# A norm's gain folded into the weights it feeds, on Pool, and Pool's additions and products handed to VectorE

## The chip, the cores and the metric

The kernel runs on one core of a Trainium2 chip. Its time is device microseconds from the first to the last instruction of one execution. The profile names the engines: PE is TensorE's matrix multiply, PEld its weight loads, DVE is VectorE, ACT is ScalarE, POOL is GpSimd ("Pool" below), SP is SyncE, which issues most of the DMAs.

## The reference: what is computed

A bidirectional encoder with two layers; S = 1024 tokens, D = 1024, a hidden width of 2816, all in fp32. Each layer mixes tokens (a Fourier group, windowed attention, attention on a memory), adds the normed result to x, and then runs a gated feed-forward block:

```python
y = jnp.concatenate([...], axis=-1) @ w_out[l]
x = x + _rmsnorm(y, g_post_mix[l])

h = _rmsnorm(x, g_pre_ffn[l])                   # x * rsqrt(mean(x*x) + eps) * g
gate, up = jnp.split(h @ w_ffn_in[l], 2, axis=-1)
f = (jax.nn.silu(gate) * up) @ w_ffn_out[l]
x = x + _rmsnorm(f, g_post_ffn[l])
```

## The kernel before

Every operand of a matmul is split into a high and a low part in a reduced fp32 format (`split`, L151 a cast on ACT for the high part, L152 a subtraction on DVE for the low one), and a product is formed from three matmuls. The two large products of the feed-forward block, "ffn_in" (h @ w_ffn_in) and "ffn_out", are done by a scheme with seven block products in place of eight: rows of x and columns of weights are cut in two, sums and differences of the blocks are multiplied, and results are added up.

**From the mixer to ffn_in (the transition).** The last stage of the mixer goes over eight token tiles of 128 rows, t = 0 to 7. `out` multiplies by w_out ("mo"), adds the parts (L1041 on DVE, with a factor `grs` from Pool), forms the residual (L337 and L338 on DVE, L337 multiplying by the row g_post_mix) and norms the row: L289 squares and sums it on ACT, L291 stores x to DRAM, two small Pool operations (L210 `nrsv`, L212 `nrs`) make the factor r, and L294 on DVE computes x * r * g_pre_ffn. Both gains are rows of 1024 values that a DMA spreads over all partitions, 512 KB each, at slots 48 and 52 of the arena. `Blocks.tile` then transposes the row on PE ("hTp", L1066), ACT copies the result (L1067), and `Blocks.sum` and `Blocks.last` build the block sums on DVE (L1084, L1096, L1097) and their splits. Blocks 2 and 4 need only token tiles 0 to 3, the others need tiles 4 to 7 too.

**ffn_in.** For each of 11 pairs p of hidden blocks there are two "quads", the gate's and the up's, each of seven products (names qy, qz, qx, qw; L1137, 12 matmuls of 512 columns each) in the order 2, 4, 5, 1, 6, 7, 3. `Quad.load` brings two raw tiles (512 KB each) of w_ffn_in; `weights` forms a sum of two parts of them on DVE (L1127) and splits it. The ring of split weight tiles holds eight. The raw tiles of pair 0 lie at slots 32, 0, 16 and 20, those of the later pairs at 44, 48, 52 and 56, and so a load waits for what lay there. `step` collects the products: ACT copies one out of PSUM (L1142), Pool adds to it (L1157) or subtracts from it (L1163), DVE does the sums with an operand in PSUM (L1158, L1169, L1172, L1173). `up_out` multiplies the up quad by silu of the gate quad (four L1189) and forms sums for ffn_out (L1199, L1201, L1203), which go to DRAM ("actd"). In all pairs but the last, Pool does two of the L1189, two of the L1199 and the L1203. `scaled` (L342), which multiplies a weight tile by one column of factors on Pool, is there already for the weights of other stages.

Every engine has one queue of instructions. Their order is set by a scheduler when the kernel is built, from its own estimates of times, so it shifts around an edit.

Of the kernel before, what the change touches and what calls it, by code (L numbers as in the profile page):

```python
# [11 lines left out]
F32 = mybir.dt.float32  # L12
# [3 lines left out]
AF = mybir.ActivationFunctionType  # L16
ALU = mybir.AluOpType
AX = mybir.AxisListType

P = 128  # L20
D = 1024
S = 1024
NT = S // P
NK = D // P
# [44 lines left out]
def tile_encoder(ctx: ExitStack, tc: tile.TileContext, T, C, out):  # L69
# [51 lines left out]
    def run(k, n, step):  # L121
        return Ring(*[k + i * step for i in range(n)])
# [40 lines left out]
                self.i += 1  # L163


    const = cp.tile([P, 1376], F32, name="const")
    used = [0]

    def cst(*shape):
# [28 lines left out]

    ggT = cst(DEPTH * NK)
    gpT = cst(DEPTH * NK)  # L200
    rx = cst(NT)
    nsink = cst(DEPTH, 8)
    psink = cst(DEPTH, 8)
# [11 lines left out]
    def gain(row, g):  # L215
        nc.sync.dma_start(g, row.partition_broadcast(P))
        return g
# [6 lines left out]
        nc.scalar.copy(dst, pt)  # L224

    def prep():
        tmp = run(6, 10, 1)
        gains_T(ggT, T["g_grp"], tmp(P))
        nc.sync.dma_start(psink, T["sink"].rearrange("l h -> (l h)").partition_broadcast(P).rearrange("p (l h) -> p l h", l=DEPTH))
        nc.vector.tensor_scalar_mul(nsink, psink, -1.0)  # L230

        pi = tmp(P, dt=I32)[:NT]
        nc.sync.dma_start(pi, T["positions"].rearrange("o (t p) -> (o t) p", p=P))
        pf = tmp(P)[:NT]
        nc.vector.tensor_copy(pf, pi)
        pp_ = ps([NT], "posT")
        nc.tensor.transpose(pp_, pf, ident[:NT, :NT])
        pos = sm(NT, "pos")
        nc.vector.tensor_copy(pos, pp_)
        invf = tmp(HD // 2)  # L240
        nc.sync.dma_start(invf, C["invf"].partition_broadcast(P))
        H = HD // 2
        shp = [NT, H]
        ang = tmp(*shp)
        nc.vector.tensor_tensor(
            out=ang, in0=pos[:, :, None].to_broadcast([P, NT, H]),
            in1=invf[:, None, :].to_broadcast([P, NT, H]), op=ALU.mult,
        )


        BIG = 1.5 * 2.0 ** 23
        two_pi = 2 * math.pi
        p_parts, p_rest = _bits_split(two_pi * 4096, [7] * 6)
        q_parts, q_rest = _bits_split(two_pi, [12] * 3)

        def count(src, unit):
            n = tmp(*shp)
            nc.vector.tensor_scalar(out=n, in0=src, scalar1=1.0 / unit, scalar2=BIG, op0=ALU.mult, op1=ALU.add)
            nc.vector.tensor_scalar_sub(n, n, BIG)
            return n  # L260

        def less(dst, n, part, src):
            nc.vector.scalar_tensor_tensor(out=dst, in0=n, scalar=-part, in1=src, op0=ALU.mult, op1=ALU.add)

        n1 = count(ang, two_pi * 4096)
        for part in p_parts[:3]:
            less(ang, n1, part, ang)
        est = tmp(*shp)
        less(est, n1, sum(p_parts[3:]), ang)
        n2 = count(est, two_pi)  # L270
        less(ang, n2, q_parts[0], ang)
        less(ang, n1, p_parts[3], ang)
        less(ang, n2, q_parts[1], ang)
        less(ang, n1, p_parts[4], ang)
        less(ang, n1, p_parts[5], ang)
        less(ang, n2, q_parts[2], ang)
        lim = float(np.nextafter(np.float32(math.pi), np.float32(0)))
        nc.vector.tensor_scalar(out=ang, in0=ang, scalar1=lim, scalar2=-lim, op0=ALU.min, op1=ALU.max)
        nc.scalar.activation(SS[:, :, H:HD], ang, AF.Sin)
        mag = tmp(*shp)  # L280
        nc.vector.scalar_tensor_tensor(out=mag, in0=ang, scalar=-1.0, in1=ang, op0=ALU.mult, op1=ALU.max)
        nc.scalar.activation(CC, mag, AF.Sin, bias=halfpi[:, 0:1], scale=-1.0)
        nc.vector.tensor_scalar_mul(SS[:, :, 0:H], SS[:, :, H:HD], -1.0)


    def norm_x(x, g, h=None, keep=None):

        ss = sm(1, "nss")
        nc.scalar.activation(junks(D // 2).bitcast(BF16) if h is None else h, x, AF.Square, accum_out=ss)  # L289
        if keep is not None:  # L290
            nc.scalar.dma_start(keep, x)  # L291
        h = x if h is None else h
        r = rsqrt_mean(ss, D, 1, "nrs")
        nc.vector.scalar_tensor_tensor(out=h, in0=x, scalar=r[:, 0:1], in1=g, op0=ALU.mult, op1=ALU.mult)  # L294
        return h

    def token_scale(x, t):
# [188 lines left out]
    class Mix:  # L486
# [525 lines left out]

        def out_gains(self):
            self.gpost = gain(T["g_post_mix"][self.l], at(48, D))
            self.gffn = gain(T["g_pre_ffn"][self.l], at(52, D))
            junks.ks, sqs.ks, es_ring.ks = (58,), (56, 56), (36, 39, 42, 45)
            self.prepped, self.xf = {}, {}

# [11 lines left out]
        def out(self, t, x1):  # L1030

            x, f = self.xf.pop(t)
            (hi, lo), rs = self.prepped.pop(t)
            for n in range(2):
                ns = slice(n * 512, n * 512 + 512)
                pt = ps([512], "mo")
                acc = Acc(pt, 4)
                for i in range(4):
                    w = self.woa[2 + i]
                    acc.add(hi[:, i], lo[:, i], w[0][:, ns], w[1][:, ns])  # L1040
                nc.vector.scalar_tensor_tensor(  # L1041
                    out=f[:, ns], in0=pt, scalar=rs[:, 0:1], in1=f[:, ns], op0=ALU.mult, op1=ALU.add
                )
            residual(x, f, self.gpost)
            return norm_x(x, self.gffn, f, x1)

# [52 lines left out]
    class Quad:  # L1101


        def __init__(self, l, c0, hb):
            self.hb, self.c0 = hb, c0
            self.w = T["w_ffn_in"][l]

        def load(self):
            self.raw = []
            for kg in range(2):  # L1110
                r = qws(4, 2, P)
                nc.sync.dma_start(
                    r, self.w[kg * 512 : kg * 512 + 512, self.c0 : self.c0 + 256].rearrange("(k p) (j c) -> p k j c", p=P, c=P)
                )
                self.raw.append(r)

        def weights(self, i):
# [27 lines left out]
        def step(self, i):  # L1145

            if i == 2:
                self.y = ps([512], "qy", "pT")
                self.product(self.y, 2, True)
                self.s2 = self.snap(self.y)  # L1150
            if i == 4:
                self.product(self.y, 4, False)
            if i == 5:
                self.z = ps([512], "qz", "av")
                self.product(self.z, 5, True)
                self.v = self.snap(self.z)
                nc.gpsimd.tensor_tensor(out=self.v, in0=self.v, in1=self.s2, op=ALU.add)  # L1157
                nc.vector.tensor_tensor(out=self.s2, in0=self.y, in1=self.v, op=ALU.subtract)  # L1158
            if i == 1:
                self.x = ps([512], "qx", "sc")  # L1160
                self.product(self.x, 1, True)
                self.s1 = self.snap(self.x)
                nc.gpsimd.tensor_tensor(out=self.s1, in0=self.v, in1=self.s1, op=ALU.subtract)  # L1163
            if i == 6:
                self.w6 = ps([512], "qw", "pd")
                self.product(self.w6, 6, True)
            if i == 7:
                self.product(self.x, 7, False)
                nc.vector.tensor_tensor(out=self.s2, in0=self.x, in1=self.s2, op=ALU.add)  # L1169
            if i == 3:  # L1170
                self.product(self.z, 3, False)
                nc.vector.tensor_tensor(out=self.s1, in0=self.z, in1=self.s1, op=ALU.subtract)  # L1172
                nc.vector.tensor_tensor(out=self.s1, in0=self.w6, in1=self.s1, op=ALU.add)  # L1173
                self.out = (self.s2, self.z, self.y, self.s1)
# [8 lines left out]

    def up_out(q, g, actd, p):

        V, G = nc.vector, nc.vector if p == NFF // 2 - 1 else nc.gpsimd
        a = [acts(512) for _ in range(4)]
        for i, c in enumerate(q.out):
            (G if i in (0, 3) else V).tensor_tensor(out=a[i], in0=c, in1=g[i], op=ALU.mult)  # L1189
        a11, a21, a12, a22 = a  # L1190

        def put(i, s):
            nc.sync.dma_start(actd[i - 1, p], s)

        put(3, a11)
        put(4, a22)
        for i, x, y, eng in ((1, a11, a22, G), (2, a21, a22, V), (5, a11, a12, G)):
            s = acts(512)
            eng.tensor_tensor(out=s, in0=x, in1=y, op=ALU.add)  # L1199
            put(i, s)  # L1200
        V.tensor_tensor(out=a21, in0=a21, in1=a11, op=ALU.subtract)  # L1201
        put(6, a21)
        G.tensor_tensor(out=a12, in0=a12, in1=a22, op=ALU.subtract)  # L1203
        put(7, a12)

    def quads(l, p, hb):
# [297 lines left out]
```

## Time and profile before

| | before |
|---|---|
| runs, us | 2087.84, 2090.29, 2091.57 (median 2090.29) |
| span of the profiled execution, us | 2089.2 |
| mean granted TensorE clock | 0.981 |
| busy: PE, DVE, ACT, POOL, us | 1994.7, 1578.8, 1069.9, 713.1 |
| ffn_in, layer 0 and layer 1, us from the start | 424 to about 843, 1454 to about 1868 |
| transition, layer 0 and layer 1 | about 394 to 424, 1421 to 1454 |

The profiled execution has no other time than its span, which lies within the runs. Times below are microseconds from the span's start. A line number such as L294 is the line of the kernel before; "x44" counts instructions, and in rows of a timeline "[0.44 <-POOL grs L962]" is the idle time of the engine just before, with what ended it.

### The profile page before, as it was taken

The page shows a single profiled execution, that of the slowest core. Times are in us where ns is not written, and L with a number is a line of the kernel's source. Part 1 is how long each engine was busy: PE and PEld are TensorE (multiplying, and loading weights), DVE is VectorE, ACT ScalarE, POOL GpSimd, SP SyncE. Part 2 cuts the span into 40 slices and gives each one's busy share as a digit, 9 for nine tenths or more (in the row PEclk, how much of TensorE's full clock was granted, in tenths as well). Part 3 has the DMA queues.
Part 4 walks back from the last instruction along what each step waited for, and adds up shares of the span by engine and source line. Part 5 has one row for each costly group of instructions (what it writes and reads, how often), then busy time and mean ns, then how long its engine had stood idle before and what let it go on. Part 6 is the DMA issues. An engine that isn't in the chain of part 4 may idle for free.

```text
span 2089.2 us, 28535 instructions
## 1 busy us (share of the span) xinstructions
PE 1994.7 (95%) x9587; PEld 1646.5 (79%) x9587; DVE 1578.8 (76%) x2540; ACT 1069.9 (51%) x2270; POOL 713.1 (34%) x819
## 2 busy tenths in 40 slices
PE   7998999799999999999999979997999999989998
PEld 6876787578888888887788768775788888878886
DVE  5558767898787877778867686579878787778767
ACT  6467777654333333544555677675433333345441
POOL 4344435433333423002523544453343342320002
PEclk9999999999999999999999999998999999999999
DMA  6111132423232333879831122233233232269874
GB/s 211 51 51 61 56 112 91 162 71 101 97 120 87 126 96 116 312 271 328 279 133 45 48 66 86 77 134 118 86 104 114 86 131 96 92 210 343 303 261 151
DMA packets 173347, 286.48 MB, mean 137 GB/s; under 512 B 15464, under 2 KB 73360, under 8 KB 173200
## 3 DMA queue, kind: packets, MB, share of 16 engines
q1 hardware_dynamic: 165136, 265.78, 37.9%
q10 hardware_dynamic: 8064, 18.88, 2.3%
q8 instruction: 75, 1.23, 0.2%
q14 instruction: 72, 0.59, 0.1%
HBM read 218.02 MB, written 66.58 MB: 136 GB/s over the span
## 4 chain that ended last, share of the span: by engine, by line
PE 74%; DVE 9%; DMA 7%; ACT 5%; issue 3%; POOL 2%; SPq 0%; DVEq 0%; ACTq 0%; POOLq 0%
PE fo L1270 13%; PE qx L1137 11%; PE qy L1137 10%; PE qz L1137 10%; PE mo L162 7%; PE qw L1137 5%; PE kvp L162 4%; DVE arena_r L152 3%; PE qp L162 3%; DMA arena_f<-actd 3%; PE zT L162 2%; PE pT L798 1%; ACT arena_r L151 1%; DMA arena_f<-in_w_ffn_out 1%; PE sc L761 1%
## 5 line engine op out<-in xcount | busy, mean ns | idle before, releaser
L151 ACT CAST arena_r<-arena_f 128x512 fp32r<-128x512 f32 (+1 forms) x780 | 443.7, 591 | 632.6 <-PE qz L1137 119.9
L152 DVE TENSOR_TENSOR arena_r<-arena_f,arena_r 128x512 fp32r<-128x512 f32 (+1 forms) x676 | 509.4, 774 | 148.1 <-ACT arena_r L151 136.8
L1270 PE MATMUL fo<-arena_r 128*128 128x512 f32 x1848 | 425.1, 391 | 8.7 <-ACT arena_r L151 7.3
L1270 PEld LDWEIGHTS fo<-arena_r 128*128 128x128 f32 x1848 | 346.6, 188 | 82.4 <-ACT arena_r L151 8.1
L1137 PE MATMUL qy<-arena_r 128*128 128x512 f32 x1056 | 261.9, 397 | 22.3 <-ACT arena_r L151 12.5
L1137 PEld LDWEIGHTS qy<-arena_r 128*128 128x128 f32 x1056 | 201.7, 192 | 66.6 <-ACT arena_r L151 13.3
L1127 DVE TENSOR_TENSOR arena_f<-arena_f 128x512 f32<-128x512 f32 x220 | 205.9, 939 | 8.9 <-issue 2.4
L1137 PE MATMUL qz<-arena_r 128*128 128x512 f32 x704 | 196.6, 389 | 1.1 <-DVE arena_r L152 1.1
L1157 POOL TENSOR_TENSOR arena_f<-arena_f 128x512 f32<-128x512 f32 x44 | 73.9, 1679 | 310.2 <-ACT arena_f L1142 310.2
L1137 PEld LDWEIGHTS qz<-arena_r 128*128 128x128 f32 x704 | 132.1, 188 | 28.9 <-DVE arena_r L152 1.5
L152 POOL TENSOR_TENSOR arena_r<-arena_f,arena_r 128x256 fp32r<-128x256 f32 (+2 forms) x104 | 87.0, 842 | 129.5 <-ACT arena_r L151 84.4
L1137 PE MATMUL qx<-big,arena_r 128*128 128x512 f32 x528 | 127.1, 389 | 1.7 <-ACT arena_f L1142 1.7
L1137 PE MATMUL qx<-arena_r 128*128 128x512 f32 x528 | 127.9, 389 | 0.5 <-ACT arena_r L151 0.5
L1137 PE MATMUL qw<-arena_r 128*128 128x512 f32 x528 | 128.3, 389 | 0.0
L1189 POOL TENSOR_TENSOR arena_f<-arena_f 128x512 f32<-128x512 f32 x40 | 66.7, 1667 | 159.7 <-DVE arena_f L1169 122.4
L1137 PEld LDWEIGHTS qx<-big,arena_r 128*128 128x128 f32 x528 | 99.0, 188 | 22.6 <-ACT arena_f L1142 2.1
L1137 PEld LDWEIGHTS qx<-arena_r 128*128 128x128 f32 x528 | 99.1, 188 | 21.4 <-ACT arena_r L151 0.9
L1137 PE MATMUL qz<-big,arena_r 128*128 128x512 f32 x352 | 115.7, 389 | 0.0
L1137 PEld LDWEIGHTS qw<-arena_r 128*128 128x128 f32 x528 | 99.1, 188 | 20.6
L210 POOL TENSOR_SCALAR rrsv<-rss 128x1 f32<-128x1 f32 x32 | 13.6, 424 | 267.6 <-ACT arena_f L323 210.0
L162 PE MATMUL mo<-big,arena_r 128*128 128x512 f32 x384 | 102.2, 406 | 0.8 <-ACT arena_f L1001 0.8
L162 PE MATMUL mo<-arena_r 128*128 128x512 f32 x384 | 100.7, 403 | 0.9 <-POOL arena_r L152 0.6
(228 smaller groups left out, 3518.3 us busy)
## 6 DMA issues: line engine op xcount, KB each, us to landing
arena_f<-in_w_ffn_out SPq DMA_DIRECT2D x264, 256.0 KB, 4.6
arena_f<-in_w_ffn_in SPq DMA_DIRECT2D x88, 512.0 KB, 3.7
actd<-arena_f SPq DMA_DIRECT2D x154, 256.0 KB, 3.7
arena_f<-actd SPq DMA_DIRECT2D x154, 256.0 KB, 4.5
arena_f<-in_w_in SPq DMA_DIRECT2D x40, 256.0 KB, 3.0
arena_f<-in_x SPq DMA_DIRECT2D x16, 512.0 KB, 5.3
arena_f<-in_w_out SPq DMA_DIRECT2D x32, 256.0 KB, 2.7
pmd<-arena_f ACTq DMA_DIRECT2D x32, 256.0 KB, 2.0
```

Of the source, the lines that this page charges most:

```text
L151: nc.scalar.copy(hi, src)
L152: return (lo_eng or nc.vector).tensor_tensor(out=lo, in0=src, in1=f32(hi), op=ALU.subtract)
L162: mm(self.dst, a, b, start=self.i == 0, stop=self.i == self.n - 1)
L210: nc.gpsimd.tensor_scalar(out=v, in0=ss, scalar1=1.0 / n, scalar2=EPS, op0=ALU.mult, op1=ALU.add)
L761: mm(pt, lhs, self.kst[g][i][:, k0 * P : k1 * P], start=i == 0, stop=i == 1)
L798: nc.tensor.transpose(pT[:, h, :], es_[h // 2][:, h % 2, j * P : j * P + P], ident)
L1127: nc.vector.tensor_tensor(out=s, in0=a, in1=b, op=op)
L1137: mm(pt, a, b, start=start and n == 0, stop=n == 11, skip_group_check=not start)
L1157: nc.gpsimd.tensor_tensor(out=self.v, in0=self.v, in1=self.s2, op=ALU.add)
L1189: (G if i in (0, 3) else V).tensor_tensor(out=a[i], in0=c, in1=g[i], op=ALU.mult)
L1270: mm(pt, ab[:, 0, x, sl], ab[:, 1, y], start=new and first and j == 0, stop=last and j == 2, skip_group_check=not new)
```

## The change

The gain g_pre_ffn no longer multiplies the normed rows. It is brought once, transposed to columns (`gfT`), and Pool multiplies each raw tile of w_ffn_in with it, in four operations of 128x256 a tile (88 tiles, 352 operations). The norm's row is multiplied by r alone, on Pool (`norm_rows`). The g_pre_ffn row at slot 52 is no longer loaded. All tensor-tensors of ffn_in that Pool did are on DVE: 44 of L1157, 44 of L1163, 40 of L1189, 40 of L1199 and 20 of L1203. In the changed kernel lines after 296 have moved by 10 to 12 (L1127 is L1139 there, L1157 is L1169, and `scaled` is L353).

```diff
+    gfT = cst(DEPTH * NK)
...
+        gains_T(gfT, T["g_pre_ffn"], tmp(P))
...
+    def norm_rows(x, h, keep):
+
+        ss = sm(1, "nss")
+        nc.scalar.activation(h, x, AF.Square, accum_out=ss)
+        nc.scalar.dma_start(keep, x)
+        r = rsqrt_mean(ss, D, 1, "nrs")
+        nc.gpsimd.tensor_scalar(out=h, in0=x, scalar1=r[:, 0:1], scalar2=1.0, op0=ALU.mult, op1=ALU.mult)
+        return h
...
-            self.gffn = gain(T["g_pre_ffn"][self.l], at(52, D))
...
-            return norm_x(x, self.gffn, f, x1)
+            return norm_rows(x, f, x1)
...
+                for k in range(4):
+                    scaled(r[:, k], gfT, self.l * NK + 4 * kg + k)
...
-                nc.gpsimd.tensor_tensor(out=self.v, in0=self.v, in1=self.s2, op=ALU.add)
+                nc.vector.tensor_tensor(out=self.v, in0=self.v, in1=self.s2, op=ALU.add)
...
-                nc.gpsimd.tensor_tensor(out=self.s1, in0=self.v, in1=self.s1, op=ALU.subtract)
+                nc.vector.tensor_tensor(out=self.s1, in0=self.v, in1=self.s1, op=ALU.subtract)
...
-        V, G = nc.vector, nc.vector if p == NFF // 2 - 1 else nc.gpsimd
+        V = nc.vector
         a = [acts(512) for _ in range(4)]
         for i, c in enumerate(q.out):
-            (G if i in (0, 3) else V).tensor_tensor(out=a[i], in0=c, in1=g[i], op=ALU.mult)
+            V.tensor_tensor(out=a[i], in0=c, in1=g[i], op=ALU.mult)
...
-        for i, x, y, eng in ((1, a11, a22, G), (2, a21, a22, V), (5, a11, a12, G)):
+        for i, x, y in ((1, a11, a22), (2, a21, a22), (5, a11, a12)):
...
-        G.tensor_tensor(out=a12, in0=a12, in1=a22, op=ALU.subtract)
+        V.tensor_tensor(out=a12, in0=a12, in1=a22, op=ALU.subtract)
```

How the edit changes the order of instructions is shown at layer 0's transition. Pool's queue before, from token tile 7's factor `grs` to the first operations of ffn_in (`nrsv` and `nrs` belong to a norm, `rrsv` and `rrs` to a residual):

```order
L962 TENSOR_TENSOR grs_585_3991<-ms_584_3989,const_77 128x1
L210 TENSOR_SCALAR nrsv_592_4032<-nss_591_4029 128x1
L212 TENSOR_TENSOR nrs_593_4034<-nrsv_592_4032,const_77 128x1
L210 TENSOR_SCALAR rrsv_601_4096<-rss_600_4094 128x1
L212 TENSOR_TENSOR rrs_602_4098<-rrsv_601_4096,const_77 128x1
L210 TENSOR_SCALAR nrsv_604_4105<-nss_603_4102 128x1
L212 TENSOR_TENSOR nrs_605_4107<-nrsv_604_4105,const_77 128x1
L1157 TENSOR_TENSOR arena_f_73<-arena_f_73 128x512 x2
L1163 TENSOR_TENSOR arena_f_73<-arena_f_73 128x512 x2
```

And after the change (L353 is a scaling of a raw tile's quarter, L305 the norm's row of a token tile):

```order
L353 TENSOR_SCALAR arena_f_73<-arena_f_73,const_77 128x256 x4
L211 TENSOR_SCALAR nrsv_593_4035<-nss_592_4032 128x1
L213 TENSOR_TENSOR nrs_594_4037<-nrsv_593_4035,const_77 128x1
L305 TENSOR_SCALAR arena_f_73<-arena_f_73,nrs_594_4037 128x1024
L353 TENSOR_SCALAR arena_f_73<-arena_f_73,const_77 128x256 x4
L211 TENSOR_SCALAR rrsv_602_4099<-rss_601_4097 128x1
L213 TENSOR_TENSOR rrs_603_4101<-rrsv_602_4099,const_77 128x1
L353 TENSOR_SCALAR arena_f_73<-arena_f_73,const_77 128x256 x12
L211 TENSOR_SCALAR nrsv_605_4108<-nss_604_4105 128x1
L353 TENSOR_SCALAR arena_f_73<-arena_f_73,const_77 128x256 x4
L213 TENSOR_TENSOR nrs_606_4110<-nrsv_605_4108,const_77 128x1
L305 TENSOR_SCALAR arena_f_73<-arena_f_73,nrs_606_4110 128x1024
```

Between token tile 6's norm and token tile 7's there now stand 20 scalings; the last four of the twelve wait for a load into the slot that held the g_post_mix row, and the four behind `nrsv` for one into slot 20.

PE's queue before, from token tile 7's transposes to the first products that need them (hTp_612 and hTp_613 are token tile 7's two halves, qy_608 and qy_611 the first products of the two quads):

```order
L1137 MATMUL qy_608_4136<-arena_r_72 128x512 x22
L1137 MATMUL qy_611_4191<-arena_r_72 128x512 x2
L1066 MATMUL hTp_612_4232<-const_77,arena_f_73 128x128 x4
L1066 MATMUL hTp_613_4238<-const_77,arena_f_73 128x128 x4
L1137 MATMUL qy_611_4191<-arena_r_72 128x512 x10
L1137 MATMUL qz_617_4278<-arena_r_72 128x512
L1137 MATMUL qw_619_4315<-arena_r_72 128x512
L1137 MATMUL qz_617_4278<-arena_r_72 128x512 x11
L1137 MATMUL qx_618_4297<-arena_r_72 128x512
L1137 MATMUL qy_611_4191<-arena_r_72 128x512 x12
```

And after:

```order
L1149 MATMUL qy_609_4147<-arena_r_72 128x512 x22
L1149 MATMUL qy_612_4210<-arena_r_72 128x512 x2
L1076 MATMUL hTp_613_4251<-const_77,arena_f_73 128x128 x4
L1149 MATMUL qy_612_4210<-arena_r_72 128x512 x10
L1076 MATMUL hTp_614_4257<-const_77,arena_f_73 128x128 x4
L1149 MATMUL qw_620_4334<-arena_r_72 128x512
L1149 MATMUL qy_612_4210<-arena_r_72 128x512 x12
L1149 MATMUL qw_620_4334<-arena_r_72 128x512 x2
L1149 MATMUL qz_618_4297<-arena_r_72 128x512
L1149 MATMUL qw_620_4334<-arena_r_72 128x512 x9
```

The second qy product of the second quad, 12 matmuls, now stands right behind the first matmul that needs token tile 7, ahead of the bulk of qz and qw.

More of the change, by code (lines that the diff above doesn't have):

```diff
@@ L163, in add @@
                 self.i += 1
-    const = cp.tile([P, 1376], F32, name="const")
+    const = cp.tile([P, 1392], F32, name="const")
     used = [0]
@@ L226, in prep @@
     def prep():
-        tmp = run(6, 10, 1)
+        tmp = run(6, 11, 1)
         gains_T(ggT, T["g_grp"], tmp(P))
+        gains_T(gfT, T["g_pre_ffn"], tmp(P))
         nc.sync.dma_start(psink, T["sink"].rearrange("l h -> (l h)").partition_broadcast(P).rearrange("p (l h) -> p l h", l=DEPTH))
@@ L1104, in __init__ @@
         def __init__(self, l, c0, hb):
-            self.hb, self.c0 = hb, c0
+            self.hb, self.c0, self.l = hb, c0, l
             self.w = T["w_ffn_in"][l]
@@ L1196, in up_out @@
         put(4, a22)
-        for i, x, y, eng in ((1, a11, a22, G), (2, a21, a22, V), (5, a11, a12, G)):
+        for i, x, y in ((1, a11, a22), (2, a21, a22), (5, a11, a12)):
             s = acts(512)
-            eng.tensor_tensor(out=s, in0=x, in1=y, op=ALU.add)
+            V.tensor_tensor(out=s, in0=x, in1=y, op=ALU.add)
             put(i, s)
```

## The prediction

> **What bounds the kernel now.** I read the page first: the busy time of each engine.
>
> ```profile
> span 2089.2 us, 28535 instructions
> PE 1994.7 (95%) x9587; PEld 1646.5 (79%) x9587; DVE 1578.8 (76%) x2540; ACT 1069.9 (51%) x2270; POOL 713.1 (34%) x819
> ```
>
> TensorE is busy 95% of the span, VectorE 76%, Pool 34%. PE is idle for 2089.2 − 1994.7 = 94.5 us in all, so the first question is whether those idle us lie where the change works. The windows view answers by stage: two stretches inside ffn_in, and the two short transitions from the mixer's output rows to ffn_in (columns: window, its length, then busy us and instruction count of PE, weight loads, DVE, ACT, Pool, the granted clock).
>
> ```profile
> 394.00:424.00 30.00, 15.12 (x57) 11.05 (x55) 28.83 (x45) 16.48 (x30) 9.18 (x7) 0.83 0.41 138
> 450.00:830.00 380.00, 380.00 (x1678) 314.74 (x1678) 301.00 (x357) 140.57 (x244) 140.36 (x91) 1.00 0.32 107
> 1421.00:1454.00 33.00, 19.47 (x68) 14.11 (x67) 30.78 (x47) 19.24 (x36) 8.63 (x6) 0.74 0.39 128
> ```
>
> In ffn_in PE has no idle time at all in 380 us, while DVE has 79 us to spare. In the transitions it is the reverse: PE works 15.12 of 30 us and 19.47 of 33 us, and DVE 28.83 and 30.78. So ffn_in is bound by PE, the transitions by DVE and the chain of the norms, and only about 14.9 + 13.5 us of PE idle time can be won or enlarged there.
>
> **ffn_in itself: moved tensor-tensors and new scalings.** The timeline of the PE gives the pace, those of DVE and Pool show why the two interfere.
>
> ```profile
> 608.72 2.88 PE L1137 MATMUL qz<-arena_r 128*128 128x512 f32 x12
> 611.44 2.88 PE L1137 MATMUL qx<-arena_r 128*128 128x512 f32 x12
> 608.08 0.68 DVE L1173 TENSOR_TENSOR arena_f<-qw,arena_f 128x512 f32<-128x512 f32 x1
> 608.68 0.68 DVE L1127 TENSOR_TENSOR arena_f<-arena_f 128x512 f32<-128x512 f32 x1
> 609.39 1.67 DVE L152 TENSOR_TENSOR arena_r<-arena_f,arena_r 128x512 fp32r<-128x512 f32 x1
> 610.98 1.78 DVE L1199 TENSOR_TENSOR arena_f<-arena_f 128x512 f32<-128x512 f32 x1
> 608.84 1.67 POOL L1189 TENSOR_TENSOR arena_f<-arena_f 128x512 f32<-128x512 f32 x1 [1.55 <-DVE arena_f L1173]
> 610.59 1.62 POOL L1199 TENSOR_TENSOR arena_f<-arena_f 128x512 f32<-128x512 f32 x1
> ```
>
> A product starts every 611.44 − 608.72 = 2.72 us; a pair of hidden blocks has two quads of seven, 14 × 2.72 = 38.1 us. DVE's 128x512 operations start 608.68 − 608.08 = 0.60 us apart while Pool is idle; beside a Pool tensor-tensor the same operation takes 1.67 to 1.78. In the 380 us window that is 380/38.1 = 10.0 pairs, so before the change DVE spends 301.00/10 = 30.1 us on 35.8 operations a pair, of which 35.8 × 0.60 = 21.5 us is the work and 8.6 us the contention. The prices of what moves, by line and shape (busy us in all, mean ns of one):
>
> ```profile
> L1157 POOL TENSOR_TENSOR arena_f<-arena_f 128x512 f32<-128x512 f32 x44 | 73.9, 1679 | 310.2 <-ACT arena_f L1142 310.2
> L1189 POOL TENSOR_TENSOR arena_f<-arena_f 128x512 f32<-128x512 f32 x40 | 66.7, 1667 | 159.7 <-DVE arena_f L1169 122.4 <-DVE arena_f L1173 34.2 <-DMA actd<-arena_f 3.1
> L1163 POOL TENSOR_TENSOR arena_f<-arena_f 128x512 f32<-128x512 f32 x44 | 63.6, 1446 | 54.5 <-ACT arena_f L1142 53.1
> L1199 POOL TENSOR_TENSOR arena_f<-arena_f 128x512 f32<-128x512 f32 x40 | 59.2, 1483 | 3.0
> L1203 POOL TENSOR_TENSOR arena_f<-arena_f 128x512 f32<-128x512 f32 x20 | 34.3, 1717 | 0.0
> L785 POOL TENSOR_SCALAR arena_f<-arena_f,rden 128x256 f32<-128x256 f32 x32 | 15.6, 506 | 14.4 <-DVE rden L782 11.5 <-ACT arena_f L834 2.6 <-DVE es L778 0.3
> L785 POOL TENSOR_SCALAR arena_f<-arena_f,rden 128x384 f32<-128x384 f32 x96 | 57.1, 613 | 21.5 <-ACT arena_r L151 7.6 <-DVE rden L782 5.9 <-ACT arena_f L335 3.3
> 964.00 2.40 POOL L342 TENSOR_SCALAR arena_f<-arena_f,const 128x256 f32<-128x256 f32 x2 [1.02 <-DMA arena_f<-in_w_in]
> 964.65 0.88 DVE L152 TENSOR_TENSOR arena_r<-arena_f,arena_r 128x512 fp32r<-128x512 f32 x1
> ```
>
> Pool loses 188 tensor-tensors worth 297.7 us, nine a pair. DVE takes them at 0.60 each, 5.4 us a pair. Pool gains 16 scalings of 128x256 a pair. The nearest rows are L785 of that shape, 0.51 us mean where DVE is not streaming, and the two scalings of 964.00, 2.40/2 = 1.2 us each while DVE streams; beside those, a DVE operation took 0.88 in place of 0.68, so 0.2 more. DVE a pair: 21.5 + 5.4 + 16 × 0.2 = 30.1 us. That is what it was, out of 38.1; if each scaling stopped DVE for its whole 0.51, it would be 35.1, still below. So ffn_in's price is taken as 0: the cover is PE's 38.1 us a pair and the eight weight tiles that may stand ready ahead of it, 8 × 2.72 = 21.8 us. Pool's 16 scalings take 8 to 19 us of the same 38.1. The change also adds a wait to DVE's queue: L1157 and L1163, now on DVE, wait for ACT's copy of a product, and the weight sums and splits queued behind them wait too. Before, L1158 stood in that queue waiting for Pool's L1157, so the wait is not new in kind, and the same 21.8 us covers it.
>
> The Trainium skill, in "SBUF — State Buffer", section "Who interferes with whom", says that DVE and GpSimd share one pair of ports as an exclusive lock, so that a tensor-tensor with both inputs in SBUF and a Pool operation block each other whole. By it every scaling would stop DVE for all of its time, and the pair would come to the 35.1 us just given; the two rows at 964 do not bear out the whole of that, since DVE lost 0.2 us there and Pool waited instead.
>
> **The transition in layer 0.** Here are the chain's rows: the last token tile's residual, the load, the norm, and the first products that need that tile.
>
> ```profile
> 386.06 1.48 DVE L1041 SCALAR_TENSOR_TENSOR arena_f<-mo,grs,arena_f 128x512 f32<-128x512 f32 x2 [0.44 <-POOL grs L962]
> 404.42 1.28 DVE L337 SCALAR_TENSOR_TENSOR arena_f<-arena_f,rrs 128x1024 f32<-128x1024 f32 x1
> 405.35 5.07 DMA arena_f<-in_w_ffn_in
> 412.20 2.51 POOL L210 TENSOR_SCALAR nrsv<-nss 128x1 f32<-128x1 f32 x1 [7.89 <-ACT arena_f L289]
> 414.79 0.55 POOL L212 TENSOR_TENSOR nrs<-nrsv,const 128x1 f32<-128x1 f32 x1
> 415.37 1.28 DVE L294 SCALAR_TENSOR_TENSOR arena_f<-arena_f,nrs 128x1024 f32<-128x1024 f32 x1 [0.71 <-POOL nrs L212]
> 418.30 0.60 PE L1066 MATMUL hTp<-const,arena_f 128*128 128x128 f32 x4
> 419.58 0.69 DVE L1084 TENSOR_TENSOR arena_f<-big,big 128x512 f32<-128x512 f32 x1
> 422.60 0.39 PE L1137 MATMUL qw<-arena_r 128*128 128x512 f32 x1
> 424.04 2.83 PE L1137 MATMUL qz<-arena_r 128*128 128x512 f32 x11 [1.06 <-DVE arena_r L152]
> ```
>
> Removed from DVE: L294, 1.21 us of its pace each. The rows of its order from the second half of token tile 6's L1041 (ended 387.54) to the first sum of the last tile's transposes (L1084 at 419.58) come to 43 operations before and 42 after. At 0.60 for 512 wide, 1.21 for L294 and L337, 1.14 for L338, 0.70 for L1041 and 0.07 for the mean, that is 29.6 us before and 27.2 after: three L294 go (−3.6), two more weight sums and one more split come (+1.8), and one L1084 moves past the end (−0.6). It took 32.0 before, so DVE waited 2.4; with as much waiting and 8 × 0.2 for scalings it is through at 387.54 + 27.2 + 2.4 + 1.6, about 418 to 419.
>
> Added on Pool: the last token tile's norm is queued behind scalings. Four of them need the tile that goes where the g_post_mix row lay; it can be loaded only when L337 has read that row for the last time, at 404.42 + 1.28 = 405.7, and with 5.07 us for the load it is there at 410.8. Then follow on Pool four scalings, nrsv, four scalings, nrs, and the norm row. Up to DVE's end at about 418 I price a scaling at 1.2 (DVE is busy 28.83 of 30 us here, which is nearest to the 964.00 row): six, to 418.0; two more at 0.51, 419.0; nrsv and nrs at 0.55 each and the 128x1024 row, an estimate from the two L785 shapes, 0.51 + 768/128 × (0.61 − 0.51) = 1.15: 421.3. In the rows above it is 419.58 − 418.30 = 1.3 from the transposes to the sum; sum and cast of 0.69 or less each add 1.3. The first product of the last tile starts at 423.9, against 422.60: +1.3. PE's order has a whole product of qy left behind it there, 2.72 us, in which the splits are made, so the wait of 1.06 goes: +0.2 us.
>
> Bounds: all eight at 0.51 give 410.8 + 4.1 + 2.25 + 2.6 = 419.8, so −2.8 − 1.06 = −3.9. All eight at 1.2, nrsv starved as at 412.20 (2.51) and the norm row at twice its time, give 428.4, so +5.8 − 1.06 = +4.7. The g_pre_ffn row is not loaded any more (512 KB), which only lets one raw tile come earlier: 0.
>
> **The transition in layer 1**, by the same steps:
>
> ```profile
> 1415.53 0.74 DVE L1041 SCALAR_TENSOR_TENSOR arena_f<-mo,grs,arena_f 128x512 f32<-128x512 f32 x1
> 1431.53 1.28 DVE L337 SCALAR_TENSOR_TENSOR arena_f<-arena_f,rrs 128x1024 f32<-128x1024 f32 x1
> 1432.53 4.67 DMA arena_f<-in_w_ffn_in
> 1446.92 0.69 DVE L1084 TENSOR_TENSOR arena_f<-big,big 128x512 f32<-128x512 f32 x1 [0.74 <-ACT big L1067]
> 1449.97 0.39 PE L1137 MATMUL qw<-arena_r 128*128 128x512 f32 x1
> 1450.87 0.51 PE L1137 MATMUL qx<-arena_r 128*128 128x512 f32 x1 [0.51 <-ACT arena_r L151]
> ```
>
> DVE's rows come to 28.4 us before, 26.6 after; it is through at about 1446. The load lands at 1432.81 + 4.67 = 1437.5. Seven scalings at 1.2 reach 1445.9, one at 0.51 1446.4, then 2.25 and 2.6: 1451.3 against 1449.97, +1.3, less the 0.51 wait: +0.8. Bounds −4.0 and +4.6, worked out alike.
>
> **The ends.**
>
> ```profile
> 4.57 0.25 PE L223 MATMUL ggp<-const,arena_f 16*128 16x16 f32 x1 [4.57 <-DMA arena_f<-in_g_pre_mix]
> 1874.55 2.08 PE L1270 MATMUL fo<-arena_r 128*128 128x512 f32 x4 [5.41 <-ACT arena_r L151]
> ```
>
> The prologue gets one more such transpose, its copy and a small load: +0.2 (0 if hidden, +2 if the load delays those behind it on SP's queue). At layer 1's entry to ffn_out PE waits 5.41; its last pair's tensor-tensors were on DVE already, so 0, between −3 and +3.
>
> **Sum.** 0 + 0.2 + 0.8 + 0.2 + 0 = +1.2, on 2089.2 us of the profiled execution 2090.4. The runs (2087.84, 2090.29, 2091.57) have their median 1.1 above that execution, so I forecast 2090.29 + 1.2 = 2091.5.
>
> **Rivals.**
> 1. Pool runs its scalings in DVE's gaps and the norm comes early: the lower bounds, −3.9 − 4.0 + 0.2 = −7.7, 2082.6. For it: the mean of L785 is 0.51, and the three L294 that leave DVE open gaps. Against: DVE is 96% busy there.
> 2. Slower: Pool starves in front of the last tile's norm. Place: the eight scalings, nrsv and norm row; price: 4.7 + 4.6 + 0.2 = +9.5, 2099.8; it decides once a scaling takes over about 1.0 us in DVE's stream to the end. For it: nrsv took 2.51 at 412.20, scalings 1.2 at 964.00. Against: DVE's rows run out near 418, and Pool is then alone.
> 3. DVE becomes the bound of ffn_in. It takes over 38.1 us a pair if a scaling costs it more than (38.1 − 26.9)/16 = 0.70 us; at 0.8 that is 1.6 us a pair, 20 pairs, +32, 2122. Against: the highest row-backed price is 0.51, the nearest 0.2.
>
> The Trainium skill's "Perfetto Trace Analysis", section "Optimizing Scalar/DVE Operations", warns that moving work between DVE and GpSimd "might not help", since they share the port; it names rival 2's mechanism, and the 1.67 beside 0.68 in ffn_in agrees that there is one.
>
> **How the numbers follow.** A measurement of this kernel can tell about 0.2%, 4.2 us. I give the forecast (within 4.2 us of no change) 0.45, rival 1 0.25, rival 2 0.25 and rival 3 0.05: faster 0.25, same 0.45, slower 0.30. The range reaches from rival 1's 2082 to rival 2's 2099.8 with 3 us for layer 1's entry, 2103; the likeliest case's own range is 2087 to 2095.
>
> **What would show it.** In the profile after: PE still busy for all of 450 to 830; DVE's sum there within some us of 301, its tensor-tensors back at 0.68 mostly; L305 near 1.15 us, or 2 and more if Pool starves; eight scalings and nrsv between the last raw tile's landing and the last L305; PE's idle time in the transitions within 4 us of 14.9 and 13.5. Wrong would be a PE with gaps in ffn_in (rival 3), or first products of the last tile that shift by more than 4 us.

## The result, and the profile after

The changed kernel took 2105.26 us in the median of four runs (2103.48 to 2108.79), against 2090.93 for the kernel before (the three runs given above and a fourth): a ratio of 1.0066, interval 1.0048 to 1.0083. It is 14 us slower, and above the upper end of my range, 2103. Two executions that took far longer than the rest, one of scale_act (5094.82 us) and one of the kernel before beside one_ts (2507.83 us), are left out of the intervals below.

The profiled execution is 12.7 us longer than the one before. Its page, and the windows of ffn_in in layer 0 and of the two transitions (columns as before):

```profile
span 2101.9 us, 28933 instructions
PE 2000.0 (95%) x9588; PEld 1650.0 (79%) x9588; DVE 1562.3 (74%) x2712; ACT 1076.0 (51%) x2271; POOL 742.4 (35%) x999
394.00:430.00 36.00, 17.57 (x53) 13.59 (x53) 30.02 (x41) 15.66 (x29) 29.51 (x32) 0.67 0.32 102
457.00:830.00 373.00, 373.00 (x1647) 308.86 (x1646) 288.04 (x438) 138.66 (x237) 129.96 (x144) 1.00 0.33 106
1429.00:1464.00 35.00, 11.45 (x39) 8.20 (x39) 25.47 (x35) 12.34 (x22) 29.24 (x33) 0.70 0.27 93
```

In ffn_in PE still has no gap in 373 us, and DVE does 438 operations there in 288 us. What has changed is Pool in the transitions: it was busy 9.18 of 30 us, and is now busy 29.51 of 36. To see where the 12.7 us are, I cut each profiled execution at the end of the last mo product, at the first and the last fo product of each layer, and took differences to the kernel before. "Transition + ffn_in" runs from the last mo to the first fo. Of ffn_in's 1848 matmuls, all but the first 120 take PE 391.8 us in each layer (391.8 and 392.2 before), so a change in this stretch is one of the transition.

| us, against the kernel before | span | transition + ffn_in, layer 0 | layer 1 | everything else |
|---|---|---|---|---|
| the changed kernel | +12.7 | +7.7 | +7.8 | −2.8 |

So both transitions pay, by the same amount, and together more than the whole loss. The amounts are not made up alike. These are the two stretches, of the kernel before and after the change, layer 0 and then layer 1 (columns as above):

```profile
394.50:834.48 439.98, 425.06 (x1865) 350.92 (x1865) 356.37 (x443) 173.95 (x302) 158.74 (x101) 0.99 0.31 104
393.29:840.99 447.70, 428.88 (x1868) 353.70 (x1867) 352.03 (x534) 176.37 (x304) 160.17 (x176) 0.97 0.32 102
1421.13:1863.54 442.41, 427.21 (x1865) 351.50 (x1865) 357.65 (x447) 177.40 (x311) 155.15 (x100) 0.98 0.32 107
1428.65:1878.82 450.17, 426.27 (x1864) 351.56 (x1865) 354.81 (x540) 178.62 (x308) 162.88 (x177) 0.97 0.32 103
```

In layer 0 PE's idle time rises from 14.92 to 18.82 us, by 3.9, and its busy time by 3.8: half of that layer's loss is matmuls that take longer. In layer 1 the idle time rises from 15.20 to 23.90, by 8.7, and the busy time falls by 0.9. Here is PE in the two transitions after the change (idle time and its end in brackets):

```profile
406.18 1.22 PE L1149 MATMUL qy<-arena_r 128*128 128x512 f32 x2 [12.56 <-ACT arena_r L151]
414.80 4.61 PE L1149 MATMUL qy<-arena_r 128*128 128x512 f32 x12 [1.98 <-ACT arena_f L1154]
423.67 1.22 PE L1149 MATMUL qy<-arena_r 128*128 128x512 f32 x2 [4.26 <-ACT arena_r L151]
429.85 0.47 PE L1149 MATMUL qw<-arena_r 128*128 128x512 f32 x1
1437.78 1.22 PE L1149 MATMUL qy<-arena_r 128*128 128x512 f32 x2 [9.13 <-ACT arena_r L151]
1458.57 1.22 PE L1149 MATMUL qy<-arena_r 128*128 128x512 f32 x2 [10.44 <-ACT arena_r L151]
1463.16 1.12 PE L1076 MATMUL hTp<-const,arena_f 128*128 128x128 f32 x4 [3.37 <-POOL arena_f L305]
```

In the kernel before, the first qy of each layer started after these waits:

```profile
399.76 1.22 PE L1137 MATMUL qy<-arena_r 128*128 128x512 f32 x2 [5.25 <-ACT arena_r L151]
1428.51 1.22 PE L1137 MATMUL qy<-arena_r 128*128 128x512 f32 x2 [7.27 <-ACT arena_r L151]
```

The long waits, 12.56, 4.26, 9.13 and 10.44 us, end with ACT's cast of a weight tile. Not all of them are loss, since the kernel before waited as well, at other places. How much later than before a matmul of ffn_in starts, counted from the last mo:

| us later than before | 1st (first quad) | 13th | 25th (second quad) | 49th |
|---|---|---|---|---|
| layer 0 | +7.6 | +2.3 | +7.0 | +7.7 |
| layer 1 | +1.8 | −3.4 | +5.9 | +9.8 |

The first quad starts late in layer 0, but by its second product (the 13th matmul) most of that is made up. What stays is lost from the second quad on: its first product waits 4.26 and 10.44 us. What ACT and DVE waited for at that time, and what Pool did, is shown by the timelines of these engines:

```profile
392.98 4.95 POOL L353 TENSOR_SCALAR arena_f<-arena_f,const 128x256 f32<-128x256 f32 x4
401.53 3.22 POOL L353 TENSOR_SCALAR arena_f<-arena_f,const 128x256 f32<-128x256 f32 x4
406.52 11.83 POOL L353 TENSOR_SCALAR arena_f<-arena_f,const 128x256 f32<-128x256 f32 x9
418.33 1.39 POOL L353 TENSOR_SCALAR arena_f<-arena_f,const 128x256 f32<-128x256 f32 x3
419.80 0.19 POOL L211 TENSOR_SCALAR nrsv<-nss 128x1 f32<-128x1 f32 x1
420.08 1.85 POOL L353 TENSOR_SCALAR arena_f<-arena_f,const 128x256 f32<-128x256 f32 x4
422.54 1.67 POOL L305 TENSOR_SCALAR arena_f<-arena_f,nrs 128x1024 f32<-128x1024 f32 x1
404.78 0.69 DVE L1139 TENSOR_TENSOR arena_f<-arena_f 128x512 f32<-128x512 f32 x1 [1.29 <-POOL arena_f L353]
404.78 1.34 ACT L151 CAST arena_r<-arena_f 128x512 fp32r<-128x512 f32 x2 [4.09 <-POOL arena_f L353]
421.96 0.69 DVE L1139 TENSOR_TENSOR arena_f<-arena_f 128x512 f32<-128x512 f32 x1 [3.96 <-POOL arena_f L353]
421.96 1.66 ACT L151 CAST arena_r<-arena_f 128x512 fp32r<-128x512 f32 x3 [7.22 <-POOL arena_f L353]
1444.51 16.46 POOL L353 TENSOR_SCALAR arena_f<-arena_f,const 128x256 f32<-128x256 f32 x15
1461.98 1.12 POOL L305 TENSOR_SCALAR arena_f<-arena_f,nrs 128x1024 f32<-128x1024 f32 x1
```

Pool works through 24 scalings from 392.98 to 421.93, with only the small operations and one row of the norms between them. A scaling's price depends on DVE. Of the twelve that start at 406.52, the first nine run beside DVE's stream, at 11.83/9 = 1.31 us each. DVE runs dry at 418.00, and the last three take 1.39/3 = 0.46 each, as do the four at 420.08.

Behind these scalings stand the weights that PE needs at once: DVE's weight sum and ACT's casts, at 404.78 for the first quad and at 421.96 for the second. The four at 420.08 belong to pair 0 (the tile in slot 20), and scalings of pair 1 stand ahead of them. Behind them too stands the last token tile's norm, whose row L305 ends at 424.2, where L294 had ended at 416.7. In layer 0 PE has no idle time from 423.67 on, so there it was the weights that it waited for and not the norm. In layer 1 there is one run of 15 scalings, 16.46 us, and PE waits for both: 10.44 us for the weights and then 3.37 us for the norm's row.

### The profile page after: what moved, and what is told of

Same layout as the page of the kernel before. It is cut to its first block, busy times and chain, and to the rows that moved or that the text cites. A ratio compares the mean times of both kernels' runs of the same rounds, so it can differ in the third digit from the quotient of the medians.

```text
span 2101.9 us, 28933 instructions
## 1 busy us (share of the span) xinstructions
PE 2000.0 (95%) x9588; PEld 1650.0 (79%) x9588; DVE 1562.3 (74%) x2712; ACT 1076.0 (51%) x2271; POOL 742.4 (35%) x999
## 4 chain that ended last, share of the span: by engine, by line
PE 83%; DVE 4%; POOL 4%; DMA 3%; ACT 3%; issue 2%; SPq 0%; DVEq 0%; POOLq 0%; ACTq 0%
PE fo L1282 17%; PE qx L1149 11%; PE qz L1149 11%; PE qy L1149 11%; PE mo L162 7%; PE qw L1149 6%; PE kvp L162 4%; PE qp L162 3%; POOL arena_f L353 2%; PE zT L162 2%; PE pT L809 2%; PE sc L772 2%; DVE arena_r L152 1%; PE av L824 1%; PE av L817 1%
## 5 line engine op out<-in xcount | busy, mean ns | idle before, releaser
L152 DVE TENSOR_TENSOR arena_r<-arena_f,arena_r 128x512 fp32r<-128x512 f32 (+1 forms) x676 | 472.1, 720 | 155.2 <-ACT arena_r L151 149.9
L353 POOL TENSOR_SCALAR arena_f<-arena_f,const 128x256 f32<-128x256 f32 (+1 forms) x384 | 343.7, 912 | 585.3 <-DMA arena_f<-in_w_ffn_in 426.0
L1149 PE MATMUL qy<-arena_r 128*128 128x512 f32 x1056 | 266.3, 400 | 39.4 <-ACT arena_r L151 36.4
L1139 DVE TENSOR_TENSOR arena_f<-arena_f 128x512 f32<-128x512 f32 x220 | 155.5, 710 | 18.7 <-POOL arena_f L353 16.3
L211 POOL TENSOR_SCALAR rrsv<-rss 128x1 f32<-128x1 f32 x32 | 12.7, 397 | 299.8 <-ACT arena_f L334 251.0
L1263 DVE TENSOR_TENSOR arena_f<-arena_f 128x512 f32<-128x512 f32 x110 | 78.9, 722 | 32.5 <-DMA arena_f<-in_w_ffn_out 31.7
```

The costliest lines, as they stand in the source:

```text
L152: return (lo_eng or nc.vector).tensor_tensor(out=lo, in0=src, in1=f32(hi), op=ALU.subtract)
L353: nc.gpsimd.tensor_scalar(out=raw, in0=raw, scalar1=g[:, k : k + 1], scalar2=1.0, op0=ALU.mult, op1=ALU.mult)
L1139: nc.vector.tensor_tensor(out=s, in0=a, in1=b, op=op)
L1149: mm(pt, a, b, start=start and n == 0, stop=n == 11, skip_group_check=not start)
L1263: nc.vector.tensor_tensor(out=s, in0=x, in1=y, op=op)
```

## The experiments

Theory Q: the scalings queued on Pool in the transitions are the loss. Rivals: the moved tensor-tensors (M), the norm's row on Pool (R), the scheduler's other order (O). Every edit is scheduled anew when it is built, so some shift of order comes with each of them. "To before" is the difference of medians to the kernel before, run beside it on the same chip; the intervals are of the ratio to it.

| | median, us | to before, us | ratio to before (interval) | layer 0 | layer 1 | everything else |
|---|---|---|---|---|---|---|
| tt_only | 2088.68 | −1.6 | 0.9985 (0.9974–0.9996) | +0.9 | −0.4 | −3.3 |
| fold_only | 2110.17 | +19.9 | 1.0091 (1.0074–1.0108) | +8.4 | +8.1 | +2.7 |
| no_scale_p01 | 2086.46 | −3.8 | 0.9976 (0.9965–0.9987) | −1.2 | −2.0 | −3.9 |
| row_dve | 2099.62 | +9.4 | 1.0045 (1.0029–1.0060) | +8.1 | +4.3 | −3.2 |
| no_scale_p1 | 2095.49 | +5.8 | 1.0027 (1.0015–1.0038) | +4.7 | +1.6 | −4.9 |
| no_scale_p0 | 2091.53 | +1.8 | 1.0012 (0.9998–1.0026) | +0.3 | +3.3 | −6.5 |
| narrow | 2095.38 | +5.7 | 1.0027 (1.0017–1.0038) | +2.7 | +2.5 | −1.6 |
| copy_gain | 2094.35 | +4.7 | 1.0028 (1.0017–1.0038) | −0.2 | −1.1 | +6.0 |
| one_tt | 2106.29 | +15.5 | 1.0083 (1.0060–1.0106) | +10.9 | +6.8 | +1.5 |
| one_ts | 2098.07 | +9.1 | 1.0035 (1.0022–1.0048) | +3.4 | −1.2 | +5.5 |
| scale_dve | 2100.02 | +9.2 | 1.0053 (1.0033–1.0073) | +4.2 | +3.8 | +0.5 |
| scale_act | 2084.77 | −6.0 | 0.9970 (0.9952–0.9987) | +2.4 | −3.7 | −2.3 |

The three right-hand columns are differences of one profiled execution each to that of before (transition + ffn_in of each layer, then the rest of the span).

**The tensor-tensors alone.** The kernel before, with

```diff
-                nc.gpsimd.tensor_tensor(out=self.v, in0=self.v, in1=self.s2, op=ALU.add)
+                nc.vector.tensor_tensor(out=self.v, in0=self.v, in1=self.s2, op=ALU.add)
...
-        V, G = nc.vector, nc.vector if p == NFF // 2 - 1 else nc.gpsimd
+        V, G = nc.vector, nc.vector
```

and L1163 likewise.

> Only the tensor-tensors of ffn_in move from Pool to VectorE; the gain stays in the norm. Theory Q (the scalings queued on Pool in the two transitions hold up the norms, the first weights and so PE): no change to the kernel before, -3 to +3 us. Rival M (the moved tensor-tensors: VectorE's queue now waits for ACT's copies at the start of ffn_in): most of the +14 us, +8 to +14. Both: PE stays busy all through ffn_in, and VectorE's 128x512 operations there go back to 0.68 us.

It was faster by 0.15%, so rival M is out: this half of the change costs nothing. In this execution the gain is not in the transitions or ffn_in; a part of it lies behind them. At layer 1's entry to ffn_out PE waited 5.41 us before, and here

```profile
1871.00 9.26 PE L1270 MATMUL fo<-arena_r 128*128 128x512 f32 x38 [1.82 <-ACT arena_r L151]
```

**The fold alone.** The changed kernel with the old `up_out`, L1157 and L1163 on Pool again.

> Only the gain moves into the weights (scalings and the norm's row on Pool); the tensor-tensors stay on Pool as before. Theory Q: the loss is here, +10 to +18 us over the kernel before, each stretch from the last mo to the first fo longer by 6 to 9 us. Rival M: -2 to +4. A second rival, B (Pool now has both, 9 tensor-tensors and 16 scalings a pair, and becomes late in ffn_in): more than +30 us.

The whole loss is here, +8.4 and +8.1 in the transitions; at +19.9 us it is more than that of the whole change, and 2 us above the range given. Rival B is out: with both on Pool, PE has only two gaps in the rest of ffn_in, 1.34 us at 487.59 and 0.20 at 1528.91.

**No scaling in the first two pairs.**

```diff
-                for k in range(4):
+                for k in range(4 if self.c0 % DFF >= 4 * P else 0):
                     scaled(r[:, k], gfT, self.l * NK + 4 * kg + k)
```

> The changed kernel with the scaling of the weights left out for the hidden blocks of pairs 0 and 1, whose raw tiles arrive during the transitions; all later pairs are scaled as in the changed kernel (so the gain is missing in those two pairs). Theory Q: the loss goes, -4 to +3 us against the kernel before. Rival R (the norm's row on Pool is what is slow: L305 behind other Pool work in VectorE's stream) : +6 to +12 stays. Rival O (the scheduler's other order of weights and sums): +6 to +12 stays.

Without them the kernel is faster than before by 0.24%, although L305 stays on Pool and pairs 2 to 10 are scaled there as in the changed kernel. R falls as the main cause; the loss needs the scalings of pairs 0 and 1. Rival O is not tested by itself, since DVE's order was another in this run too. Against it as the main cause stand the rows above, in which the waits end with scalings.

**The norm's row on VectorE.** `nc.vector.tensor_scalar` in `norm_rows` in place of `nc.gpsimd.tensor_scalar`.

> The changed kernel with the norm's row (x times r) on VectorE again, without the gain; scalings stay on Pool. Theory Q: nrsv and nrs still stand behind the scalings on Pool, and the first weights still wait for them, so +8 to +14 us over the kernel before stays. Rival R: back to within +-4 us of the kernel before.

+9.4 us: most of the loss stays, as Q has it, but layer 1 gets 3.5 us back. How much of that is the row's own and how much another order is not separated: Pool's run of scalings there was 13.34 us for 16, against 16.46 for 15. The row took 801 ns on DVE (mean of 16), less than L294's 1322.

**One pair at a time.** The same condition, for pair 1 alone and for pair 0 alone.

> The changed kernel without the scalings of pair 1, whose raw tiles are not needed until 38 us later but whose scalings stand ahead of the last token tile's norm; pair 0's stay. If the last norm's delay is the cost: half or more of the +14 us goes, 0 to +7 us against the kernel before. If the cost is pair 0's weights, which the first products wait for: +9 to +14 stays.

> The changed kernel without the scalings of pair 0, which the first products wait for; pair 1's stay. If pair 0's weights are the cost: -4 to +4 us against the kernel before. If the last norm's delay by pair 1's scalings is: +7 to +12 stays.

At +5.8 and +1.8 us, each run lies in the range by which the pair that it leaves out is the cost, so neither pair is all of it. In layer 0 pair 0's scalings account for most (+0.3 is left without them, +4.7 without pair 1's), in layer 1 pair 1's do (+1.6 without pair 1's, +3.3 without pair 0's). Where pair 0's scalings are gone, PE in layer 1 still waits for the norm's row behind those of pair 1:

```profile
1446.97 1.12 PE L1076 MATMUL hTp<-const,arena_f 128*128 128x128 f32 x4 [4.47 <-POOL arena_f L305]
```

So both ways of waiting count: pair 0's weights, which the first products need, and the norm behind pair 1's scalings, which nobody needs for another 38 us. The run without pair 1's scalings cannot tell the two ways apart, because in the changed kernel some of them stand ahead of pair 0's last tile as well as of the norm.

**Hardly any work in the scalings.**

```diff
-                    scaled(r[:, k], gfT, self.l * NK + 4 * kg + k)
+                    scaled(r[:, k] if self.c0 % DFF >= 4 * P else r[:, k, :, 0:4], gfT, self.l * NK + 4 * kg + k)
```

> The changed kernel with the scalings of pairs 0 and 1 cut to 8 of 256 columns (so most of the gain is missing in those pairs): as many Pool instructions, with the same waits for loads, but hardly any work. If theory Q holds because of the time that a scaling takes beside VectorE's stream (1.0 to 1.2 us each, Qd): -5 to +3 us against the kernel before. If it holds because Pool's queue stands in order behind loads that have not landed (Qo): +6 to +12 stays.

It came out between the two, at +5.7: +5.2 of +15.5 stays in the transitions, with 1/32 of the elements. Pool's timeline says why:

```profile
402.52 9.90 POOL L353 TENSOR_SCALAR arena_f<-arena_f,const 128x8 f32<-128x8 f32 x8
412.39 0.99 POOL L353 TENSOR_SCALAR arena_f<-arena_f,const 128x8 f32<-128x8 f32 x4
414.28 0.99 POOL L353 TENSOR_SCALAR arena_f<-arena_f,const 128x8 f32<-128x8 f32 x4
```

DVE ran dry at 412.28. The eight scalings of 8 columns beside its stream took 9.90 us, 1.24 each, and the eight after it 0.25 each. With 256 columns it was 1.31 and 0.46. So in the stream little of a scaling's time depends on its size. What the trace shows gone with the elements is time of the scalings outside the stream, and delay of DVE: it kept its pace of 0.60 here, where in the changed kernel many of its operations beside scalings took 0.88 in place of 0.68. Waiting for loads (Qo) is no large part in layer 0: of Pool's 4.5 us of idle time before scalings in the first of the groups below, 4.34 lie before 384.53.

**One Pool instruction for a tile.** If each instruction waits for a gap of its own, fewer and larger ones should be cheaper. First as a tensor-tensor with the gain as a broadcast operand:

```diff
+                    gb = gfT[:, k0 : k0 + 4]
+                    rr = r.rearrange("p k j c -> p k (j c)")
+                    nc.gpsimd.tensor_tensor(out=rr, in0=rr, in1=gb[:, :, None].to_broadcast([P, 4, 2 * P]), op=ALU.mult)
```

> The changed kernel with the four scalings of a raw tile of pairs 0 and 1 made one Pool tensor-tensor of 128x1024, the gain as a broadcast operand: 7 Pool instructions in place of 28 ahead of the last norm, each of some 2.7 us (L338 on Pool took 2655 ns for 128x1024 before). If what a scaling costs beside VectorE's stream is mostly the wait for a gap, paid once for each instruction (theory G): a tile takes some 3 us in place of 4.4, and +4 to +11 us over the kernel before is left of +14. If it is the work and the lock on the port (rival W): +14 to +25, since two inputs take Pool over twice as long.

Then, with that result known, as a tensor-scalar:

```diff
+                else:
+                    scaled(r.rearrange("p k j c -> p (k j c)"), gfT, k0)
```

> The changed kernel with each raw tile of pairs 0 and 1 scaled by one Pool tensor-scalar of 128x1024, with one factor for all four quarters of the tile (so the gain is wrong in those two pairs): the same elements as in the changed kernel, in 7 instructions in place of 28, with one input, unlike the 128x1024 tensor-tensor, which stopped a VectorE operation for 1.7 us. Theory G (each Pool instruction waits for its own gap in VectorE's stream, and a one-input operation then costs VectorE little): a tile takes 1.1 to 2.3 us, as the norm's row did, in place of 4.4, and -4 to +5 us against the kernel before is left of +14. Theory W (the work on the elements counts): +9 to +14 stays.

The groups of the window 385 to 425, of the changed kernel, of one_tt and of one_ts (busy us, mean ns of one, idle time before them):

```profile
L353 POOL TENSOR_SCALAR arena_f<-arena_f,const 128x256 f32<-128x256 f32 x28 | 25.1, 914 | 4.5 <-DMA arena_f<-in_w_ffn_in 4.3
```

```profile
L1132 POOL TENSOR_TENSOR arena_f<-arena_f,const 128x1024 f32<-128x1024 f32 x7 | 15.2, 2179 | 11.2 <-DMA arena_f<-in_w_ffn_in 11.2
L152 DVE TENSOR_TENSOR arena_r<-arena_f,arena_r 128x512 fp32r<-128x512 f32 x11 | 11.6, 1062 | 0.0
```

```profile
L353 POOL TENSOR_SCALAR arena_f<-arena_f,const 128x1024 f32<-128x1024 f32 x7 | 14.6, 2089 | 10.5 <-DMA arena_f<-in_w_ffn_in 10.5
L152 DVE TENSOR_TENSOR arena_r<-arena_f,arena_r 128x512 fp32r<-128x512 f32 x13 | 9.4, 744 | 0.0
```

Pool's own time fell as theory G has it, from 25.1 us to 15.2 and 14.6 for the same elements. But as a tensor-tensor it brought nothing, +15.5 us, in the range of rival W; what Pool saved DVE paid, an operation at a time:

```profile
401.53 2.32 POOL L1132 TENSOR_TENSOR arena_f<-arena_f,const 128x1024 f32<-128x1024 f32 x1
402.02 2.38 DVE L152 TENSOR_TENSOR arena_r<-big,arena_r 128x512 fp32r<-128x512 f32 x1
```

0.68 became 2.38, so DVE stood still for most of Pool's operation. That is the lock of which the Trainium skill speaks in "SBUF — State Buffer", section "Who interferes with whom": a DVE instruction with two SBUF inputs contends with a Pool instruction that reads SBUF. For these two the trace agrees. As a tensor-scalar of the same size the transitions come to +3.4 and −1.2, +2.2 in all, in the range that theory G gave; the time as a whole, +9.1 (+5 to +10 by the interval), does not, and lies at the edge of theory W's. In the profiled execution, +7.7 us, +5.5 of it lie in stages that the edit doesn't touch. So for the price of a scaling G holds, and for the time as a whole this run doesn't decide. A DVE operation beside such a tensor-scalar took 1.52 (0.68 alone):

```profile
401.94 2.07 POOL L353 TENSOR_SCALAR arena_f<-arena_f,const 128x1024 f32<-128x1024 f32 x1
403.03 1.52 DVE L1094 TENSOR_TENSOR arena_f<-big,big 128x512 f32<-128x512 f32 x1
```

**The scalings on other engines.** On VectorE (`nc.vector.tensor_scalar` for pairs 0 and 1), and on ACT:

```diff
+                        nc.scalar.activation(r[:, k], r[:, k], AF.Copy, scale=gfT[:, kk : kk + 1])
```

> The changed kernel with the scalings of pairs 0 and 1 on VectorE itself, 28 of 128x256 a layer at some 0.3 to 0.35 us by their width, so 8 to 10 us more work on VectorE, which is the bound of the transitions, but no wait for a gap and no queue on Pool ahead of the norm. Theory Q with gaps: +2 to +10 us over the kernel before, below the changed kernel's +14. If VectorE's sum of work is all that matters: +14 to +20.

> The changed kernel with the scalings of pairs 0 and 1 on ACT (28 of 128x256, some 0.36 us each, 10 us of each transition, in which ACT was busy about half). If Pool's price was that it shares with VectorE: -5 to +4 us against the kernel before. If any queue that takes the scalings in order holds up what stands behind them (here ACT's casts): +5 to +12.

VectorE pays for them with work: +7.9 in the transitions, and +9.2 as a whole, near the upper end of the range for theory Q. On ACT the kernel is faster than before by 0.30%, −6.0 us, a little beyond the range given, and 0.15% better than the tensor-tensors alone, though these two intervals overlap. Each of ACT's 64 scalings took 0.49 to 0.52 us, whatever DVE did, a tile 1.71, and every element is still scaled:

```profile
404.92 1.71 ACT L1130 ACTIVATE arena_f<-arena_f,const 128x256 f32<-128x256 f32 x4 [0.50 <-DMA arena_f<-in_w_ffn_in]
```

**The gain in the copies of the transposed rows.** No weight is scaled; ACT's copy L1077 becomes four with a factor.

> The changed kernel with the gain applied elsewhere: not to the weights, but by ACT in its copies of the transposed rows, where a feature is a partition (four copies of 128x128 with a factor in place of one of 128x512); the whole computation is kept, and Pool has no scalings in ffn_in. Theory Q: as without scalings, -8 to +1 us against the kernel before. If ACT's copies (four of some 0.25 us in place of one of 0.58) hold up the transposes instead: +1 to +8.

A miss for theory Q: the transitions are as good as it expected (−1.3), but the whole is +4.7, in the range of the other reading. In its profile the last mo ends at 398.4 in place of 394.5, and layer 0's ffn_out is 4.4 us longer. The first fits ACT's longer copies, which already run in the mixer's last stage; that was not tested, and the second is not explained.

## Why the prediction was wrong

**ffn_in at no cost: right.** PE has no gap in 457 to 830. DVE needs 288.04 us of these 373, 29.4 a pair, against my 30.1. The moved tensor-tensors cost nothing, and the Pool operations that stayed there do not reach PE.

**Price of a scaling in the transition: right.** I took 1.2 us from the row at 964.00 and 0.51 without DVE; measured were 1.31 and 0.46.

**How many of them stand in the way: the first step that failed.** My sum for a transition began when the tile in g_post_mix's slot had landed, at 410.8, with Pool free, and counted the eight scalings behind that point. I had shown in the order that 20 stood between the last two norms, and priced 8. Pool was not free: it had been working off its queue since 392.98 at a price that I knew. At 410.85 nine of the twelve were still to come, with the four behind them thirteen in place of eight, and the twelfth ended at 419.72. Where I had the last norm's row done at 421.3, it was 424.2. The first product of the last tile, at 423.9 by my sum, came at 429.85; of these 6 us only 2.9 are Pool's. The other 3 come from PE's own order, in which ten qy matmuls stand between the last tile's two groups of transposes, and these had themselves waited for their weights until 423.67. Multiplying out what the order showed, 24 scalings at my own 1.2 us are 29 us of Pool in a stretch of 30; they took 23.2.

**A wait that the sum did not have: the second.** I followed the norm alone. The first weights of ffn_in now wait for Pool too, and ACT's and DVE's queues stand behind them. I treated pair 0's scalings as something between a load and a cast, at no cost, without asking who needs them first. The runs show that this wait is the larger one: the time is lost where the second quad's first product waits for the last of these weights, 4.26 us in layer 0 and 10.44 in layer 1, and without pair 0's scalings +0.3 of layer 0's +7.7 is left.

**Matmuls that take longer.** My sum took every matmul at its old length. In layer 0 PE's busy time rose by 3.8 us, half of the loss there. Its idle time rose by 3.9 alone, within the 4 us that I had allowed, so this sign did not tell; in layer 1 it rose by 8.7 and did.

**Rival 2 had the mechanism, in another place and size.** Pool starved beside DVE ahead of the last norm, as it has it, but in the scalings before the eight that it named: the last seven took 0.46 each, nrsv 0.19 and the norm's row 1.67. It was priced at +9.5 for both transitions; they cost +15.5. Its point of decision, over about 1.0 us "in DVE's stream to the end", was met in the stream (1.31), not to the end.

**"DVE runs dry and Pool is then alone": only briefly right.** DVE did run dry at 418.00, as I had it, and stood still for 3.96 us, but because it waited for the scalings, so that its idle time was part of the loss.

**The ends.** At layer 1's entry to ffn_out I took 0, between −3 and +3; PE's wait there fell from 5.41 to 1.54, and moving the tensor-tensors alone already did that.

**What stays open.** The column "everything else" goes from −6.5 to +6.0 over kernels that differ little outside the transitions. It holds shifts of the scheduler's order and the scatter of one execution; I have not separated them. The columns of the transitions are of one execution each as well, so a difference of a few us between two experiments shows a cause only where a wait in the trace goes with it.

## What to carry to other kernels

When an edit adds instructions to a lightly used engine, multiply all that its queue holds in the tightest stretch by the price in that stretch, from the first of them on, and list who waits for each. Beside a VectorE that streams two-input operations, a small Pool instruction cost about 1.2 us here however little it did. The same work was cheapest on ACT. As few large one-input instructions it took less of Pool's time, but the kernel as a whole did not come back to its old time, and a large two-input one on Pool stopped VectorE instead. A change made of two halves can be a small gain and a larger loss: run the halves apart.

## What the runs showed of the hardware that I had not expected

A Pool scaling of 128x8 took 1.24 us beside VectorE's stream of tensor-tensors and 0.25 alone, while VectorE kept its pace of 0.60: there it is Pool that waits, for a time that depends little on its size (1.31 for 128x256). From 406.89 to 411.7 these scalings started 1.21 us apart, one for every two VectorE operations.

And matmuls can stay slow after a wait. In layer 0, after 12.56 and 1.98 us of idle time, twelve matmuls took 4.61 us, where they take 2.88 in ffn_in, with a granted clock of 0.67 over the window from 394 to 430. The first 48 matmuls of ffn_in kept PE busy for 18.66 us, against 14.75 before, at granted clocks of 0.70 and 0.84 from the last mo to their end. So a wait can cost more than its idle time. It need not: in layer 1 PE idled 8.7 us longer than before, and the same 48 took 16.00 us against 16.16, at 0.72 and 0.74. What decides it these runs do not show.
